# Delta rule: the 16x16 substitution issued on GpSimd, and diagonal blocks taken to scratch by eight small DMAs

## The chip, the core and the metric

The kernel runs on one core of a Trainium2 chip. The metric is device time in microseconds for one launch, that is, one inference step of a two-layer recurrent trunk. Engines have short names in the profile: PE is TensorE (PEld its weight loads), DVE is VectorE, ACT is ScalarE, POOL is GpSimd, SP is the engine that issues nearly all DMAs (its queue is SPq).

## The reference, cut to what matters

The step takes 2048 prompt tokens and 8 sample tokens of width 1024 through an even layer (gated linear attention beside a state-space model) and then an odd layer, the gated delta rule. Only the odd layer matters here. For each of 8 heads and each chunk of tokens it computes

```python
kk = einsum('bhik,bhjk->bhij', ki, ki)
lower = where(strict, bi[..., :, None] * kk * decay, 0.0)
sol = triangular_solve(lower + eye, rhs, left_side=True, lower=True, unit_diagonal=True)
u_v, w_k = sol[..., :DN_DV], sol[..., DN_DV:]
v_new = u_v - einsum('bhik,bhkv->bhiv', w_k, S)
o = einsum('bhik,bhkv->bhiv', qi * exp(gcum)[..., None], S) + einsum('bhij,bhjv->bhiv', scores, v_new)
S = S * exp(g_last)[..., None] + einsum('bhjk,bhjv->bhkv', ki * exp(g_last - gcum)[..., None], v_new)
```

So a unit lower triangular matrix is inverted per chunk and head, and the state S passes from chunk to chunk.

## The kernel before, in words

The 2048 tokens of the odd layer are 16 chunks of 128 tokens. Four chunks make a block (the first block also carries the 8 sample tokens), and a block is worked head by head: 4 blocks x 8 heads are 32 steps, numbered g. The kernel works with chunks of 128 where the reference has 64; the result is the same.

A step has these parts, each a Python generator that issues instructions and yields:

- `dn_dense` projects keys, queries, values and the gate for the head (matmuls `pmm` on TensorE with weights `whl` that SP loads at line 308 into a ring of four buffers), with a convolution on VectorE (line 1687) and the tail of the block kept by GpSimd (line 1680).
- `dn_prefix` loads the decays into the single buffer `gr` (line 1740, issued by SP), makes the decay matrix `E` (VectorE line 1743, GpSimd mask line 1744, ScalarE), the norms of the keys (a power on GpSimd, line 1727), and the scaled triangular matrix `MT`, 128 x 4 x 128 (line 1779). It then begins the inverse: the eight 16x16 blocks on the diagonal of `MT` are brought together for all partitions and solved by substitution.
- `dn_queries` makes the norms of the queries (lines 1726, 1727, 1815), turns the values, and scales the queries by `eg` on GpSimd (line 1831). `eg` lies in the buffer of `gr`, so the next step's load at line 1740 waits for line 1831.
- `dn_inverse` expands the solved blocks to `U` and its transpose `Tm` (lines 1841 and 1845), and doubles the block size three times, 16 to 32, 64 and 128, with small matmuls `prc` that alternate with copies on VectorE (lines 1859, 1861, 1882) and ScalarE.
- `dn_chain` passes the state `dS` through the four chunks (matmuls `pch` and `ppo`; VectorE lines 1916 and 1933), and `dn_gate` gates the result.

Between blocks `dn_entry` norms the next block's input (GpSimd products of 128x1024 at line 641), and `dn_out` multiplies by the output weights (sums at lines 2038 and 2091).

The substitution in `dn_prefix` goes as follows before the change. VectorE multiplies `MT` by a mask of diagonal blocks into `X` (line 1784, the buffer `lb`) and sums `X` over the eight blocks into `md`, 16 numbers per row and chunk (line 1786). One DMA writes `md` to scratch in DRAM (line 1788, two scratch tensors used in turn), and two DMAs read it back into two tiles LB, buffers `la` and `lb`, such that each partition holds all 16 rows of its block (line 1791). Then `u_` is filled with the unit rows (line 1794), and 15 times a row product (line 1798) and a sum (line 1800) follow, each on 128 partitions x 4 chunks x 15 down to 1 columns; each operation needs the one before it. Both are VectorE's.

What sets the order: TensorE's instructions are placed by hand. `Weave` switches between the generators and counts TensorE's time; a part that needs a result waits for a posted key and its delay (`LAT["mt"]` is 28.3 us from `MT` to the inverse). All other engines' instructions are ordered when the kernel is built, by a planner with a simulated time line and priorities (`LEAD` gives the chain and the side parts theirs), and on the chip each engine works its list strictly in that order, waiting where it must.

Of the kernel before, what the change touches and what calls it, by code (L numbers as in the profile page):

```python
# [12 lines left out]
F32 = mybir.dt.float32  # L13
# [5 lines left out]
OP = mybir.AluOpType  # L19
AX = mybir.AxisListType  # L20
# [3 lines left out]
P = 128  # L24
# [115 lines left out]
def tile_trunk(ctx, tc, A, O):  # L140
    nc = tc.nc
# [8 lines left out]
    NCG = GBLK[0][1]  # L150

    def bounds(blk):
        c0, n = blk
        first = c0 == 0
        ns = NSM if first else 0
        off = 0 if first else NSM + P * c0
        subs, c = [], 0
        o = 0
        np_ = -(-(P * n + ns) // 512)
        while c < n:  # L160
            k = -(-(n - c) // (np_ - len(subs)))
            w = P * k + (ns if c == 0 else 0)
            subs.append((o, w, c, k))
            o += w
            c += k
        return ns, off, o, subs
# [21 lines left out]
    def ptp():  # L188
        return psum.tile([P, 512], F32, tag="tp", bufs=2, name="ptp")

    def prc():
        return psum.tile([P, 512], F32, tag="rc", bufs=2, name="prc")
# [39 lines left out]
    blkd = const.tile([P, P], F32, name="blkd")  # L232
    posd = const.tile([P, 16], F32, name="posd")

    def delta_masks():
# [5 lines left out]
                                fill=0.0, base=15, channel_multiplier=-1)  # L241
        nc.vector.tensor_reduce(posd, ident.rearrange("p (b i) -> p i b", i=16), axis=AX.X, op=OP.add)

# [1077 lines left out]
    def s5_glu(sp, half):  # L1321
# [64 lines left out]
        if ns:  # L1386
# [14 lines left out]
    dp = Phase(tc, "dn", late=("Oh", "Ol", "on", "og", "kq_", "U", "Tm", "zz", "la", "lb", "xx", "ww", "sw", "so",  # L1401
                               "ktok", "vtok"))
# [313 lines left out]
    def tiles_of(n):  # L1716
        return lambda tag, bufs=1: dp.tile([P, NCG, P], F32, tag=tag, bufs=bufs, name=tag)[:, :n]

    def norms(pt, n, name):

        ss = dp.tile([P, NCG], F32, tag=name, bufs=2, name=name)[:, :n]
        for c in range(n):
            jk = dp.tile([P, P], BF16, tag="jk", bufs=1, name="jk")
            nc.scalar.activation(jk, pt[:, c * P:(c + 1) * P], AF.Square, accum_out=ss[:, c:c + 1])  # L1724
        rn = dp.tile([P, NCG], F32, tag="rn" + name, bufs=2, name="rn")[:, :n]
        nc.vector.tensor_scalar(ss, ss, 4.0 * EPS, None, op0=OP.add)
        nc.gpsimd.tensor_tensor(rn, ss, mhalf.to_broadcast([P, n]), op=OP.pow)
        return ss, rn

    def dn_prefix(dp, blk, h, g):  # L1730

        ns, off, T, subs = bounds(blk)
        n = blk[1]
        kT = dd[g][0]
        bcol, neg, bs = gates[blk]
        b3 = lambda t: t.unsqueeze(2).to_broadcast([P, n, P])
        mb = lambda m: m.unsqueeze(1).to_broadcast([P, n, P])
        T3 = tiles_of(n)
        gr = dp.tile([P, TG], F32, tag="gr", bufs=1, name="gr")
        nc.sync.dma_start(gr[:, :T], gc_d[h:h + 1, off:off + T].to_broadcast([P, T]))  # L1740
        c3 = lambda t: t[:, ns:T].rearrange("p (c t) -> p c t", t=P)
        E = T3("E")
        nc.vector.tensor_tensor(E, c3(gr), b3(bcol[:, :n, 32 + h]), op=OP.subtract)
        nc.gpsimd.affine_select(E, E, pattern=[[0, n], [1, P]], compare_op=OP.is_ge,
                                fill=-1e30, base=0, channel_multiplier=-1)
        nc.scalar.activation(E, E, AF.Exp)
        eg = gr
        nc.scalar.activation(eg[:, :T], gr[:, :T], AF.Exp)
        if ns:
            egs[g] = dp.tile([P, NSM], F32, tag="egs", bufs=2, name="egs")  # L1750
            nc.vector.tensor_copy(egs[g], eg[:, :NSM])
            weave.post(("eg", g))
        egl = dp.tile([P, NCG], F32, tag="egl", bufs=3, name="egl")[:, :n]
        nc.vector.tensor_copy(egl, c3(eg)[:, :, P - 1])

        ktok = T3("ktok", 3)
        pt = ptp()
        for c in range(n):
            pe.transpose(pt[:, c * P:(c + 1) * P], kT[:, c], ident)
        sk, rk = norms(pt, n, "sk_")  # L1760
        nc.vector.tensor_tensor(ktok, pt[:, :n * P].rearrange("p (c t) -> p c t", t=P),
                                E[:, :, P - 1:P].to_broadcast([P, n, P]), op=OP.mult)
        ivr = dp.tile([P, NCG], F32, tag="ivr", bufs=2, name="ivr")[:, :n]
        nc.vector.scalar_tensor_tensor(ivr, sk, 0.5, rk, op0=OP.mult, op1=OP.mult)
        cb = dp.tile([P, NCG], F32, tag="cb", bufs=3, name="cb")[:, :n]
        nc.vector.tensor_tensor(cb, rk, rk, op=OP.mult)
        nc.vector.tensor_tensor(cb, cb, bcol[:, :n, h], op=OP.mult)
        ncb = dp.tile([P, NCG], F32, tag="ncb", bufs=2, name="ncb")[:, :n]
        nc.vector.tensor_scalar(ncb, cb, -1.0, None, op0=OP.mult)
        keys[g] = c3(eg), E, ktok, ivr, cb, egl  # L1770
        weave.post(("keys", g))
        yield LAT["tp"]

        pk = prc()
        for c in range(n):
            pe.matmul(pk[:, c * P:(c + 1) * P], kT[:, c], kT[:, c], start=True, stop=True)
        MT = T3("MT", 2)
        for c in range(n):
            nc.vector.scalar_tensor_tensor(MT[:, c], pk[:, c * P:(c + 1) * P], ncb[:, c:c + 1],  # L1779
                                           E[:, c], op0=OP.mult, op1=OP.mult)  # L1780


        X = T3("lb")
        nc.vector.tensor_tensor(X, MT, mb(blkd), op=OP.mult)
        md = dp.tile([P, NCG, 16], F32, tag="md", bufs=1, name="md")[:, :n]
        nc.vector.tensor_reduce(md, X.rearrange("p c (b i) -> p c i b", i=16), axis=AX.X, op=OP.add)  # L1786
        w = md_d[g % 2]
        nc.sync.dma_start(w[:, :n * 16], md.rearrange("p c i -> p (c i)"))
        LB = [dp.tile([P, 8, NCG * 16], F32, tag=t, bufs=b, name="LB")[:, :, :n * 16] for t, b in (("la", 1), ("lb", 1))]
        for i in range(2):  # L1790
            nc.sync.dma_start(LB[i], bass.AP(w.tensor, w.offset + i * 8 * NCG * 16,
                                             [[16 * NCG * 16, 8], [0, 16], [NCG * 16, 8], [1, n * 16]]))
        u_ = dp.tile([P, NCG, 16], F32, tag="u_", bufs=2, name="u_")[:, :n]
        nc.vector.tensor_copy(u_, posd.unsqueeze(1).to_broadcast([P, n, 16]))
        t_ = dp.tile([P, NCG, 16], F32, tag="t_", bufs=1, name="t_")[:, :n]
        for j in range(15):
            L3 = LB[j // 8][:, j % 8].rearrange("p (c i) -> p c i", i=16)
            nc.vector.tensor_tensor(t_[:, :, j + 1:], L3[:, :, j + 1:],
                                    u_[:, :, j:j + 1].to_broadcast([P, n, 15 - j]), op=OP.mult)
            nc.vector.tensor_tensor(u_[:, :, j + 1:], u_[:, :, j + 1:], t_[:, :, j + 1:], op=OP.add)  # L1800
        mid[g] = MT, u_
        weave.post(("mid", g), LAT["mt"])

# [168 lines left out]
    def dn_sample(dp, h, kqs, eg, bs, oh, ol, zs):  # L1972
# [37 lines left out]
        nc.vector.tensor_tensor(jk, sk[:, 0], sk[:, 1], op=OP.mult)  # L2010
        nc.vector.tensor_reduce(qk, jk, axis=AX.X, op=OP.add)
        o = dp.tile([NSM, P], F32, tag="so", bufs=1, name="so")
# [225 lines left out]
    def prefixes():  # L2238
        yield "rsd", len(SBLK) - 1
        sp.close("sq")  # L2240
        gp.close("ext", "out2", "out")
        dp.open("late", "right")
        oo[GBLK[0]] = new_o()
        for g, blk, h in steps:
            if h == 0:
                yield "gates", g // NH
                columns(dp, blk, bac[blk])
            if g > 1:
                yield "prefix", g - 2
            if g > 2:  # L2250
                yield "chain", g - 3
            if g:
                yield "queries", g - 1
            yield "k", g
            yield from dn_prefix(dp, blk, h, g)
# [32 lines left out]
    a, b = LEAD  # L2288
# [34 lines left out]
```

## Time and profile before

| | |
|---|---|
| median of 3 runs | 3323.97 us (3307.7, 3323.97, 3343.99) |
| profiled execution | 3307.6 us, its span 3305.7 us, mean granted TensorE clock 0.962 |
| TensorE busy | 2975.1 us (90%), 18425 matmuls |
| VectorE busy | 2214.6 us (67%), 5715 instructions |
| ScalarE busy | 1256.0 us (38%) |
| GpSimd busy | 952.5 us (29%), 1204 instructions |
| substitution steps | 32, the first `MT` at 1742.6 us, the last `Tm` of line 1845 at 3233.1 us |

The span is from the first to the last instruction of the profiled execution; the time also has what lies around it. Busy shares are means over stages with different limits, so what a stage waits for has to be read from that stage. An arrow in a row names what ended an engine's idle time. The chain of work that ended last has 3% of the span in the loads of LB from scratch and 2% in the writes of `md`.

### The profile page before, as it was taken

Reading aid. Unit: us, or ns where it says so; the run is one execution under the profiler, and the core shown is the slowest. Engines: PE = TensorE matmul, PEld = TensorE weight load, DVE = VectorE, ACT = ScalarE, POOL = GpSimd, SP = SyncE. Lnnn points to the kernel's source line nnn. Section 1 sums busy time; section 2 is a strip of 40 time slices with the busy share of each in tenths; the row PEclk is TensorE's granted clock in tenths of the full one; section 3 lists DMA queues with packets and bytes.
Section 4 is the critical chain, followed back from the end, with each engine's and each line's share of the span. In section 5 each row is a group of like instructions: output and inputs, shape, how many; then the busy total and the mean of one; then the engine's idle time right before and its main releaser. Section 6 shows DMA issues by size and latency. Waiting matters only on the chain.

```text
span 3305.7 us, 52923 instructions
## 1 busy us (share of the span) xinstructions
PE 2975.1 (90%) x18425; PEld 2510.2 (76%) x18425; DVE 2214.6 (67%) x5715; ACT 1256.0 (38%) x3321; POOL 952.5 (29%) x1204
## 2 busy tenths in 40 slices
PE   6888899899999979879988988889999899999998
PEld 6777677677778858777778888877777688777876
DVE  7766666635535448657658888667775777757775
ACT  5343343333323223331244444434444344434442
POOL 6565344322112231330234344421111111211111
PEclk9999999999999989999998899999999999999999
DMA  7576955763563474574476566674446644474445
GB/s 215 183 221 194 299 160 151 234 214 128 179 224 125 155 266 151 177 249 130 145 236 205 158 186 200 199 255 142 132 129 195 217 129 135 128 253 142 144 128 184
DMA packets 398871, 602.94 MB, mean 182 GB/s; under 512 B 61113, under 2 KB 256556, under 8 KB 398468
## 3 DMA queue, kind: packets, MB, share of 16 engines
q1 hardware_dynamic: 398102, 598.39, 57.3%
q8 instruction: 145, 2.38, 0.3%
q10 hardware_dynamic: 502, 1.17, 0.1%
q14 instruction: 122, 1.00, 0.1%
HBM read 433.31 MB, written 166.34 MB: 181 GB/s over the span
## 4 chain that ended last, share of the span: by engine, by line
PE 29%; DVE 15%; DMA 10%; issue 3%; ACT 2%; POOL 2%; SPq 1%; DVEq 0%; POOLq 0%; ACTq 0%
PE pmm L93 20%; PE prc L93 3%; DMA LB<-md_d 3%; PE pch L93 2%; DMA md_d<-md 2%; PE ptp L97 2%; PE ppo L93 2%; DMA gr<-gc_d 1%; DVE yc L1687 1%; DVE z L1242 1%; DMA whl<-split 1%; DVE z L1232 1%; DVE z L1238 1%; DVE MT L1779 1%; DVE md L1786 1%
## 5 line engine op out<-in xcount | busy, mean ns | idle before, releaser
L93 PE MATMUL pmm<-Hh,whl 128*128 128x512 f32 (+4 forms) x5200 | 1602.7, 371 | 32.8 <-ACT Hh L643 10.4
L93 PEld LDWEIGHTS pmm<-Hh,whl 128*128 128x128 f32 x5200 | 954.2, 194 | 164.1 <-ACT Hh L643 12.0
L93 PE MATMUL pmm<-Hl,whl 128*128 128x512 f32 (+5 forms) x2640 | 941.4, 357 | 8.1 <-DVE Hl L644 5.6
L93 PEld LDWEIGHTS pmm<-Hl,whl 128*128 128x128 f32 (+1 forms) x2640 | 508.8, 193 | 58.9 <-DVE Hl L644 7.8
L93 PE MATMUL pmm<-Oh,whl 128*128 128x512 f32 (+2 forms) x1120 | 353.2, 377 | 33.2 <-DVE res L1059 11.4
L315 POOL TENSOR_TENSOR whl<-raw,whl 128x512 fp32r<-128x512 f32 (+1 forms) x176 | 229.7, 1309 | 212.4 <-ACT whl L314 160.4
L93 PEld LDWEIGHTS pmm<-Oh,whl 128*128 128x128 f32 x1120 | 209.3, 198 | 69.5 <-DVE res L1059 14.6
L1687 DVE SCALAR_TENSOR_TENSOR yc<-pre,cvec,yc 128x512 f32<-128x512 f32 (+1 forms) x288 | 229.5, 797 | 37.9 <-ACT yc L1685 34.9
L93 PE MATMUL pmm<-Ol,whl 128*128 128x512 f32 (+2 forms) x560 | 201.8, 360 | 1.4 <-DVE Ol L365 1.4
L314 ACT ACTIVATE whl<-raw 128x512 fp32r<-128x512 f32 (+1 forms) x176 | 108.1, 617 | 71.1 <-PE pmm L93 57.1
L93 PEld LDWEIGHTS pmm<-Ol,whl 128*128 128x128 f32 x560 | 111.3, 199 | 12.1 <-DVE Ol L365 2.4
L902 DVE TENSOR_TENSOR dlt<-b 128x512 f32<-128x512 f32 x112 | 89.9, 803 | 38.5 <-ACT E L909 37.5
L903 ACT ACTIVATE E<-dlt 128x256 f32<-128x256 f32 x112 | 47.4, 423 | 169.9 <-DVE dlt L902 44.4
L1680 POOL COPY halo<-pre 128x3 f32<-128x3 f32 x96 | 20.9, 217 | 298.9 <-ACT pre L1677 297.2
L93 PEld LDWEIGHTS prc<-Tm,MT 32*32 32x32 f32 (+2 forms) x1024 | 67.2, 139 | 51.1 <-DVE Tm L1882 30.1
L1677 ACT ACTIVATE pre<-pmm 128x512 f32<-128x512 f32 (+1 forms) x120 | 61.0, 510 | 115.9 <-PE pmm L93 115.8
L93 PE MATMUL pmm<-oh,whl 128*128 128x512 f32 (+3 forms) x320 | 92.4, 367 | 12.5 <-DVE res L1373 8.1
L641 POOL TENSOR_TENSOR xb<-xb,rr 128x1024 f32<-128x1024 f32 (+1 forms) x32 | 77.6, 2434 | 89.8 <-DMA xb<-xs_d 34.9
L93 PE MATMUL prc<-Tm,MT 32*32 32x32 f32 (+2 forms) x1024 | 75.5, 225 | 30.1 <-DVE Tm L1882 22.8
L1059 DVE TENSOR_TENSOR res<-pmm,res 128x512 f32<-128x512 f32 (+2 forms) x80 | 46.2, 584 | 76.6 <-PE pmm L93 55.9
L1724 ACT ACTIVATE jk<-ptp 128x128 bf16<-128x128 f32 x256 | 70.6, 276 | 67.5 <-PE ptp L97 62.8
L1951 ACT ACTIVATE jk<-ppo,rq 128x128 bf16<-128x128 f32 x128 | 46.7, 365 | 128.7 <-PE ppo L93 127.8
(1526 smaller groups left out, 6032.3 us busy)
## 6 DMA issues: line engine op xcount, KB each, us to landing
whl<-split SPq DMA_DIRECT2D x460, 512.0 KB
split<-whl SPq DMA_DIRECT2D x168, 512.0 KB
res<-xs_d SPq DMA_DIRECT2D x88, 256.0 KB
sm<-s5m SPq DMA_DIRECT2D x32, 514.0 KB
raw<-in_w_in_even SPq DMA_DIRECT2D x32, 512.0 KB
xs_d<-res SPq DMA_DIRECT2D x64, 256.0 KB
raw<-in_w_in_odd SPq DMA_DIRECT2D x32, 512.0 KB
LB<-md_d SPq DMA_DIRECT2D x64, 256.0 KB
```

Of the source, the lines that this page charges most:

```text
L93: return self.e.matmul(out, w, x, **kw)
L97: return self.e.transpose(out, x, ident)
L314: nc.scalar.activation(t[:, 0, :m], raw[:, k:k + m], AF.Copy)
L315: nc.gpsimd.tensor_tensor(t[:, 1, :m], raw[:, k:k + m], t[:, 0, :m].bitcast(F32), op=OP.subtract)
L641: nc.gpsimd.tensor_tensor(xb, xb, rr.unsqueeze(1).to_broadcast(list(xb.shape)), op=OP.mult)
L902: nc.vector.tensor_tensor(d3, b3, b3[:, :, s - 1:s].to_broadcast([P, nb_, 2 * s]), op=OP.subtract)
L903: nc.scalar.activation(E3[:, :, s:], d3[:, :, s:], AF.Exp, scale=IS)
L1059: nc.vector.tensor_tensor(res[:, o:o + w], ps, res[:, o:o + w], op=OP.add)
L1677: nc.scalar.activation(pre[:, X0 + c * P:X0 + (c + k) * P], ps[:, n0:], AF.Copy)
L1687: nc.vector.scalar_tensor_tensor(yv, pre[:, i:W - 3 + i], convw[:, ti, i:i + 1], yv, op0=OP.mult, op1=OP.add)
L1724: nc.scalar.activation(jk, pt[:, c * P:(c + 1) * P], AF.Square, accum_out=ss[:, c:c + 1])
L1951: nc.scalar.activation(jk[:rows], po[:rows, c * P:(c + 1) * P], AF.Square, scale=rq[:rows, c:c + 1], accum_out=s1[:, c:c + 1])
```

## The change

The masked product and the sum over blocks are gone. Eight DMAs, one for each group of 16 partitions, take the 16x16 diagonal blocks of the four chunks from `MT` to the scratch tensor; each moves 16 partitions x 4 chunks x 16 numbers, in pieces of 64 bytes (4 KB in all). The two loads of LB are the same. The copy that fills `u_` and the 30 operations of the substitution are issued on GpSimd. All that reads `u_`, and the rest of the kernel, is unchanged; the tiles `X` and `md` are no longer made.

```diff
-        X = T3("lb")
-        nc.vector.tensor_tensor(X, MT, mb(blkd), op=OP.mult)
-        md = dp.tile([P, NCG, 16], F32, tag="md", bufs=1, name="md")[:, :n]
-        nc.vector.tensor_reduce(md, X.rearrange("p c (b i) -> p c i b", i=16), axis=AX.X, op=OP.add)
         w = md_d[g % 2]
-        nc.sync.dma_start(w[:, :n * 16], md.rearrange("p c i -> p (c i)"))
+        for b in range(8):
+            nc.sync.dma_start(w[16 * b:16 * b + 16, :n * 16].rearrange("p (c i) -> p c i", i=16),
+                              MT[16 * b:16 * b + 16, :, 16 * b:16 * b + 16])
         LB = [dp.tile([P, 8, NCG * 16], F32, tag=t, bufs=b, name="LB")[:, :, :n * 16] for t, b in (("la", 1), ("lb", 1))]
         for i in range(2):
             nc.sync.dma_start(LB[i], bass.AP(w.tensor, w.offset + i * 8 * NCG * 16,
                                              [[16 * NCG * 16, 8], [0, 16], [NCG * 16, 8], [1, n * 16]]))
         u_ = dp.tile([P, NCG, 16], F32, tag="u_", bufs=2, name="u_")[:, :n]
-        nc.vector.tensor_copy(u_, posd.unsqueeze(1).to_broadcast([P, n, 16]))
+        nc.gpsimd.tensor_copy(u_, posd.unsqueeze(1).to_broadcast([P, n, 16]))
         t_ = dp.tile([P, NCG, 16], F32, tag="t_", bufs=1, name="t_")[:, :n]
         for j in range(15):
             L3 = LB[j // 8][:, j % 8].rearrange("p (c i) -> p c i", i=16)
-            nc.vector.tensor_tensor(t_[:, :, j + 1:], L3[:, :, j + 1:],
+            nc.gpsimd.tensor_tensor(t_[:, :, j + 1:], L3[:, :, j + 1:],
                                     u_[:, :, j:j + 1].to_broadcast([P, n, 15 - j]), op=OP.mult)
-            nc.vector.tensor_tensor(u_[:, :, j + 1:], u_[:, :, j + 1:], t_[:, :, j + 1:], op=OP.add)
+            nc.gpsimd.tensor_tensor(u_[:, :, j + 1:], u_[:, :, j + 1:], t_[:, :, j + 1:], op=OP.add)
```

## Rows read from the trace of the kernel before

**Rows 1.** Busy us by stretches: stretch, length, PE, PEld, DVE, ACT, POOL, clock, DMA.

```profile
1740.00:3306.00 1566.00, 1428.30 (x9599) 1212.40 (x9597) 1146.98 (x3166) 647.39 (x1886) 355.45 (x417) 0.96 0.55 171
1740.00:2130.00 390.00, 342.07 (x2828) 320.65 (x2827) 327.35 (x950) 174.29 (x547) 170.93 (x177) 0.93 0.61 188
2220.00:2470.00 250.00, 235.96 (x1596) 195.58 (x1595) 188.53 (x534) 104.38 (x314) 34.92 (x51) 0.99 0.47 143
```

**Rows 2.** Waits of TensorE, 1740 to 3306 us: total, times, longest.

```profile
PE pch L93 <- DVE dS L1933: 23.0, 13, 4.9
PE prc L93 <- DVE Tm L1882: 22.8, 18, 1.9
...
PE pmm L93 <- DVE yt L2091: 9.2, 10, 2.7
...
PE prc L93 <- DVE Tm L1859: 7.3, 7, 2.3
...
PE pch L93 <- DVE u__27195 L1800: 4.2, 1, 4.2
```

**Rows 3.** Tile LB: what ended its engine's standing, us and times.

```profile
  DMA LB<-md_d: 72.3, 31
```

**Rows 4.** Time line, 2270 to 2320 us: start, us, instruction, [idle before, releaser].

```profile
2279.51 0.22 DVE L1798 TENSOR_TENSOR t__23762<-LB,u__23760 128x60 f32<-128x60 f32 x1 [2.55 <-DMA LB<-md_d]
...
2280.27 0.28 DVE L1882 COPY Tm<-prc 32x128 f32<-32x128 f32 x1
...
2280.61 0.68 PE L93 MATMUL prc<-Tm,MT 64*64 64x64 f32 x8 [1.21 <-DVE Tm L1882]
```

**Rows 5.** Time lines of DVE and PE: Tm made, then first used.

```profile
1822.18 0.71 DVE L1845 STREAM_TRANSPOSE Tm<-U 128x512 f32<-128x512 f32 x1
1829.88 1.00 PE L93 MATMUL prc<-Tm,MT 128*128 128x64 f32 x8
...
2292.48 0.71 DVE L1845 STREAM_TRANSPOSE Tm<-U 128x512 f32<-128x512 f32 x1
2306.05 1.00 PE L93 MATMUL prc<-Tm,MT 128*128 128x64 f32 x8
```

**Rows 6.** Groups of DVE instructions, 1740 to 3306 us: busy us, mean ns, idle.

```profile
L1786 DVE TENSOR_REDUCE md<-lb 128x64 f32<-128x512 f32 x32 | 33.1, 1034 | 0.5
...
L1784 DVE TENSOR_TENSOR lb<-MT,blkd 128x512 f32<-128x512 f32 x32 | 23.5, 736 | 0.1
```

**Rows 7.** Busy time of line 1798 alone: stretch, length, DVE, clock, DMA.

```profile
1740.00:3306.00 1566.00, 112.64 (x480) 0.96 0.55 171
```

**Rows 8.** Time lines of POOL and DVE at the end of a block.

```profile
2475.88 7.04 POOL L641 TENSOR_TENSOR xb<-xb,rr 128x1024 f32<-128x1024 f32 x3 [1.81 <-ACT rr L1571]
...
2476.22 2.09 DVE L1798 TENSOR_TENSOR t__25812<-LB,u__25810 128x36 f32<-128x36 f32 x1
...
2480.71 2.26 DVE L1798 TENSOR_TENSOR t__25812<-LB,u__25810 128x32 f32<-128x32 f32 x1
```

**Rows 9.** Time line of SP's queue in the step of rows 4.

```profile
2273.35 0.32 SPq L1788 DMA_DIRECT2D md_d<-md  x1
...
2275.56 1.23 SPq L1791 DMA_DIRECT2D LB<-md_d  x2
```

**Rows 10.** Waits of SP's queue, 1740 to 3306 us.

```profile
SPq L308 <- PE pmm L93: 474.5, 161, 10.0
...
SPq L1740 <- POOL qT L1831: 68.0, 18, 8.8
```

**Rows 11.** Two GpSimd lines: ns min/median/max, first and last start.

```profile
L590 POOL TENSOR_TENSOR x<-q x64: 393/405/1207, 132.5 to 689.2; 128x128 f32<-128x128 f32 x64
...
L593 POOL COPY smR<-q x64: 173/184/1012, 130.8 to 680.8; 128x1 f32<-128x1 f32 x64
```

**Rows 12.** POOL's time line in the step of rows 4; DVE's standing at line 1743.

```profile
2282.97 1.28 POOL L1831 TENSOR_TENSOR qT<-qT,gr 128x512 f32<-128x512 f32 x1 [10.56 <-DVE sq__23893 L1726]
...
2289.27 0.64 POOL L1744 TENSOR_SCALAR_AFFINE_SELECT E<-E 128x512 f32<-128x512 f32 x1 [4.06 <-DVE E L1743]
...
  DMA gr<-gc_d: 29.2, 25
```

## The prediction

> **What bounds the kernel now.** I read the busy time by stretches first. The code that changes runs in the delta-rule half, 1740 to 3306 us. There TensorE is busy 1428 of 1566 us, so 138 us are all that any change off TensorE can win, 4% of the run; VectorE is busy 1147 us and GpSimd 355 us [rows 1]. The reader is to see two different parts in it: up to 2130 us (the first block of tokens) VectorE is busy 327 of 390 us and GpSimd 171, while in the steady steps (2220 to 2470 us) TensorE has 236 of 250 us and GpSimd only 35.
>
> Then the waits of TensorE, because only these are time. The largest that end with VectorE are 23.0 us for the state dS, 22.8 us for Tm at line 1882, 9.2 for the output sum, 7.3 for Tm at line 1859 and 4.2 at one place where a substitution operation was the last releaser [rows 2]: 66.5 us in these rows, of which I look for what the change can reach.
>
> The third view is the tile that the substitution reads. VectorE stood 72.3 us, in 31 of 32 steps, at its first substitution operation, until the load of LB had landed [rows 3]. VectorE works its list in order, so what is behind stands too. One step shows it: the first operation comes at 2279.51 after 2.55 us of standing, line 1882 only after it at 2280.27, and the matmuls that need Tm start at 2280.61 after a wait of 1.21 us [rows 4]. So the substitution reaches TensorE by what stands behind it on VectorE, and not by its own result: Tm from line 1845 is done at 2293.19 (2292.48 + 0.71) and first multiplied at 2306.05, 12.9 us later. In the tightest of the 32 steps the pair is 1822.89 and 1829.88, 7.0 us [rows 5].
>
> **The change part by part.** The sum is made against the profiled execution, 3307.6 us (a span of 3305.7 and 1.9 around it). The median of the three runs is 3323.97, 16.4 higher; I take the same difference off both.
>
> *Masked product and sum go.* 23.5 us and 33.1 us of VectorE [rows 6]. *Thirty small operations a step leave VectorE*, with one copy: line 1798 alone is busy 112.6 us in 480 operations, 0.235 us each [rows 7]; line 1800 has as many of like shape, so I put the whole at some 225 us. Together about 280 of VectorE's 1147 us. As busy time that is worth nothing by itself; it counts where TensorE waits for VectorE.
>
> *The standing at LB leaves VectorE.* What hangs behind it are the waits at lines 1882 and 1859, 22.8 + 7.3 = 30.1 us, and the 4.2 us one: 34 us gained. The ratio 30.1 / 72.3 = 0.42 is my price for one microsecond of standing on VectorE; I use it below.
>
> *Block ends.* There a large GpSimd product holds up VectorE: three products of 2.35 us run from 2475.88 to 2482.92, and the substitution operations on VectorE, which elsewhere last 0.2 us, last 2.09 and 2.26 us there, the first and the last of three [rows 8]. They cannot stand on VectorE any more; I take 5 us for the block ends. Gains: 39 us.
>
> *Eight small DMAs in place of one.* Issue to issue, the old one has landed and let the LB load start after 2.21 us, and that load is used 3.95 us after its issue [rows 9]. An issue costs SP 0.32 us, so eight are 2.6 us; the last should land about 2.2 us after its own issue. From MT to the substitution that adds some 2.3 us of issues and takes away 0.69 + 1.03 us of work on VectorE. The net of some 0.6 us is hidden by the 7.0 to 12.9 us above: 0. SP mostly stands for buffers of weights (line 308 waiting for TensorE, 474.5 us in all), so its 2.3 us a step are taken from that [rows 10]: 0 again, and at worst 2.3 x 32 x 0.42 = 31 us if SP's cover were gone. A gain from it I exclude: nothing waits for less.
>
> *The substitution on GpSimd.* No row has this operation there. From below: a copy of one column takes 0.184 us; from above: a product of 128 columns, twice the widest of the thirty, takes 0.405 us [rows 11]. The widths are 60 down to 4, so I take 0.30 with the gap to the next: 9 us a step (5.5 to 12.2), against the 13 us in which VectorE works through them now among other work. By its length alone it is covered by the slack, even at the upper end.
>
> The Trainium skill would price it higher. Its page "GPSIMD Engine Reference", section "4.1 Engine selection", says that two-input elementwise work belongs on VectorE and is about twice as slow on GpSimd. By it an operation would take an estimated 0.47 us, and a step 14 us. The trace does not show it so far: rows 7 and 11 leave room for 0.8 to 1.7 times.
>
> *What is queued on GpSimd behind it.* In the same stretch GpSimd multiplies the queries (line 1831, 2282.97, 1.28 us), raises the norms to a power (line 1727) and masks E for the next step (line 1744, 2289.27) [rows 12]. Line 1831 is the one that matters: it releases the only buffer gr, for which SP stands at line 1740 already (68.0 us, 18 times [rows 10]) and VectorE at line 1743 (29.2 us, 25 times [rows 12]). There is no slack: each microsecond by which line 1831 comes later stands on SP and on VectorE. Now it runs 3.5 us after LB has landed; in the new list some of the thirty will be in front of it, by the planner's order. At 0.30 us 12 of them fit in 3.5 us; if the planner puts 15 there, it is 1 us late. I take 1 us: 31 x 1 x 0.42 = 13 us lost. Bounds: 0 (all that is in front fits) and, with all thirty in front at 0.30, 9 - 3.5 = 5.5 us late, 72 us.
>
> *Both engines at SBUF together.* Rows 8 show that a VectorE operation can last until a GpSimd one is over. Ahead, each of thirty short ones can do this to VectorE: about five such meetings a step at 0.3 us would be 32 x 5 x 0.3 x 0.42 = 20 us. Against it stand the 280 us taken off VectorE. I count 0, bounds minus 16 (rival 1) and plus 20.
>
> Sum: 39 - 13 = 26 us gained; 3307.6 becomes 3282 and the median **3298 us**.
>
> **Rivals.**
> 1. *VectorE's relief thins the other waits as well.* With a quarter of its work gone, half of the waits for dS and for the output sum (23.0 + 9.2) go, 16 us, and GpSimd is never late: 39 + 16 = 55, so 3269 us. For it: VectorE at 327 of 390 us in the first block. Against: in the steady steps it has 25% of idle time and the waits are there all the same.
> 2. *Slower: the queue on GpSimd sets gr free late.* Place: line 1831, and from it SP at 1740 and VectorE at 1743. It decides from the point where 31 x lateness x 0.42 is above 39 us, which is 3.0 us. At the upper price, 0.405 us, with all but four of the thirty in front, 26 x 0.405 - 3.5 = 7 us of lateness give 91 - 39 = 52 us lost: 3376 us. For it: no slack in rows 10 and 12, and GpSimd's 171 us of 390 in the first block, to which 72 would be added. Against: line 1831 would be ordered by when its inputs are ready, between two dependent operations. The Trainium skill's page named above is on this side.
> 3. *The standing only moves*, from LB on VectorE to gr and to the norms that VectorE takes from GpSimd, and gain and loss cancel: 3324 us. For it: GpSimd stands for the same LB, with line 1831 behind it.
> 4. *The eight DMAs do not overlap*: 8 x 2.2 = 18 us in place of 2.2, 15.5 more, beyond the 12.9 us of slack by 2.6 in a usual step: 32 x 2.6 = 83 less 39, 3368 us. Against: the two loads of LB are issued back to back in 1.23 us and both are there within 3.95 [rows 9]. The Trainium skill speaks for it: "DMA: Bandwidth & Descriptors", section "Rules for kernel authors", wants many small transfers joined into one, since below 64 KB one pays mostly overhead; these are 4 KB each.
>
> **How the numbers follow.** Chances: forecast 0.32, rival 1 0.27, rival 2 0.24, rival 3 0.13, rival 4 0.04. The spread of the three runs is 1.1%, so a change within 1% (33 us) is what a measurement here can't tell from none. Faster than 3291: all of rival 1 and 0.06 of the forecast, 0.33. Slower than 3357: 0.22 of rival 2 and 0.03 of rival 4, 0.25. The rest, 0.42, is within 1%. The range goes from 3245 (rival 1 with all of the dS waits gone and a little of the rest) to 3385 (just past rival 2); beyond it I leave some 0.07 below and 0.11 above. The forecast's own range is 3285 to 3318.
>
> **What would show it.** VectorE's busy time from 1740 us on should fall from 1147 to some 860 us and GpSimd's rise from 355 to about 640; the wait for LB should be GpSimd's, TensorE's waits at lines 1882 and 1859 under 8 us together; the thirty operations at 0.2 to 0.3 us each, and Tm still 5 us or more ahead of its use. Rival 2 shows as SP's wait at 1740 well over 68 us and VectorE's at 1743 over 100; rival 3 as such waits of some 70 us beside unchanged waits of TensorE; rival 4 as the substitution beginning over 15 us after MT. The forecast is wrong if an operation on GpSimd takes over 0.4 us, or if TensorE's waits for dS grow.

## The result, and the profile after

The changed kernel takes 3360.2 us (median of 10 runs, 3347.99 to 3370.21) against 3329.31 us of before in the same comparison (10 runs): the ratio is 1.0096, with a 95% interval of 1.007 to 1.0121, some 31 us slower where the prediction had 26 us faster. The ratio is within the 1% that the prediction could not tell from none, but with ten runs each the interval excludes no change as well as any gain; the time itself lies just past 3357 us, above which the prediction had a chance of 0.25. The profiled run took 3347.99 us, its span is 3346.0 us and the mean granted clock 0.955 (before 0.962); both profiled runs are the fastest of their kernel, and lie 40.4 us apart. Lines behind the change have numbers lower by two: 1798 is now 1796, 1815 is 1813, 1831 is 1829, 1845 is 1843, 1859 is 1857, 1882 is 1880, 1916 is 1914 and 1933 is 1931.

Busy time by stretches, columns as in [rows 1]:

```profile
1740.00:3306.00 1566.00, 1417.92 (x9549) 1203.89 (x9548) 905.43 (x2073) 639.48 (x1870) 632.71 (x1403) 0.96 0.55 168
1740.00:2130.00 390.00, 333.36 (x2735) 314.50 (x2734) 262.88 (x672) 167.38 (x534) 233.78 (x422) 0.92 0.58 180
```

The work moved as intended: VectorE is busy 905 us where it was 1147, GpSimd 633 where it was 355. Nothing is gained by that alone. The waits of TensorE from 1740 us to the end (total, times, longest), to be held against [rows 2]:

```profile
PE pch L93 <- DVE dS L1931: 26.8, 18, 3.9
PE prc L93 <- DVE Tm L1843: 13.4, 4, 4.9
...
PE pmm L93 <- DVE yt L2089: 9.1, 6, 2.6
...
PE prc L93 <- DVE Tm L1857: 5.7, 5, 2.8
...
PE pch L93 <- DVE xx__28643 L1914: 3.1, 1, 3.1
...
PE pch L93 <- DVE xx__24406 L1914: 2.9, 1, 2.9
```

Of the 22.8 us at line 1882 only 0.4 are left, and line 1859 fell from 7.3 to 5.7 us: what was predicted of them came. In their place stand two others. The tiles `xx` of line 1914, of which two rows are shown, make 38.2 us together (7.3 before), and Tm of line 1843, for which TensorE had no wait before, makes 13.4 us in four. All rows of this view sum to 149.7 us after and 125.4 before, 24.3 us more.

Where the 40.4 us lie is seen when both traces are cut at the same work, the start of the first `MT` (1742.63 us before, 1751.21 after) and of the ninth, where the second block begins. TensorE's list is the same in both. Stretch, length, PE, clock, DMA; before, then after:

```profile
1742.63:3305.70 1563.07, 1425.67 (x9577) 0.96 0.55 171
1742.63:2182.23 439.60, 388.89 (x3114) 0.94 0.62 193
...
1751.21:3346.00 1594.79, 1433.18 (x9577) 0.96 0.55 168
1751.21:2208.22 457.01, 394.28 (x3114) 0.92 0.60 186
```

So 8.6 us have come up ahead of the first `MT`, where the change does nothing (mean granted clock there 0.954 after, 0.964 before). The delta rule itself is 31.7 us longer: 24.2 us in which TensorE waits and 7.5 us of its busy time. Of the 31.7, 17.4 are in the first block, at a clock of 0.92 against 0.94, and 14.3 in the three others.

What `xx` waits for is seen in VectorE's own waits:

```profile
DVE rq L1813 <- POOL rn L1727: 92.2, 27, 6.1
DVE E L1743 <- DMA gr<-gc_d: 74.7, 29, 4.8
```

Before, the first of these was 0.4 us in 2 waits, and the second 29.2 us in 25 [rows 12]. And GpSimd, at its first substitution operation (line 1796), stood until LB had landed; where VectorE had 72.3 us in 31 steps [rows 3], it has

```profile
  DMA LB<-md_d: 253.6, 32
```

One steady step shows how these belong together (time line: start, us, instruction, idle before and releaser; it is of the same kind as that of [rows 4, 9, 12], two heads further on):

```profile
2374.98 5.12 SPq L1785 DMA_DIRECT2D md_d<-MT  x8
...
2381.37 1.28 SPq L1789 DMA_DIRECT2D LB<-md_d  x2
...
2385.30 0.17 DVE L1726 TENSOR_SCALAR sq__24747<-sq__24747 128x4 f32<-128x4 f32 x1 [2.00 <-ACT jk L1724]
...
2387.07 0.30 POOL L1796 TENSOR_TENSOR t__24624<-LB,u__24622 128x60 f32<-128x60 f32 x1 [10.07 <-DMA LB<-md_d]
...
2388.58 0.28 POOL L1796 TENSOR_TENSOR t__24624<-LB,u__24622 128x52 f32<-128x52 f32 x1
...
2388.82 1.01 POOL L1727 TENSOR_TENSOR rn<-sq__24747,mhalf 128x4 f32<-128x4 f32 x1
...
2389.87 0.26 DVE L1813 TENSOR_SCALAR rq<-rn 128x4 f32<-128x4 f32 x1 [3.08 <-POOL rn L1727]
2390.04 0.34 DVE L1914 SCALAR_TENSOR_TENSOR xx__24805<-pch,neg,vtok 128x128 f32<-128x128 f32 x1
2390.07 1.27 POOL L1829 TENSOR_TENSOR qT<-qT,gr 128x512 f32<-128x512 f32 x1
...
2390.53 0.46 PE L93 MATMUL pch<-xx__24805,U 128*128 128x128 f32 x2 [0.85 <-DVE xx__24805 L1914]
...
2391.36 0.32 SPq L1740 DMA_DIRECT2D gr<-gc_d  x1
...
2395.29 0.69 DVE L1743 TENSOR_TENSOR E<-gr,bcol 128x512 f32<-128x512 f32 x1 [4.32 <-DMA gr<-gc_d]
...
2395.90 0.34 DVE L1931 SCALAR_TENSOR_TENSOR dS<-dS,egl,pch 128x128 f32<-128x128 f32 x1
...
2396.30 0.49 PE L93 MATMUL pch<-dS,kT 128*128 128x128 f32 x2 [2.08 <-DVE dS L1931]
```

The sums of the query norms are ready at 2385.47. Their power (line 1727) stands behind five substitution operations in GpSimd's list, and the first of these stands for LB until 2387.07; so it runs at 2388.82, 3.35 us after its input. Before, in the step of [rows 12], it was done at 2285.21, 0.93 us ahead of line 1815, and no `xx` stood directly behind that line:

```profile
2284.20 1.01 POOL L1727 TENSOR_TENSOR rn<-sq__23893,mhalf 128x4 f32<-128x4 f32 x1
...
2285.88 0.34 DVE L1916 SCALAR_TENSOR_TENSOR xx__23961<-pch,neg,vtok 128x128 f32<-128x128 f32 x1
2286.14 0.16 DVE L1815 TENSOR_SCALAR rq<-rn 128x4 f32<-128x4 f32 x1
```

Now VectorE, working its list in order, stands 3.08 us at line 1813, which needs it, with `xx` behind: TensorE waits 0.85 us. The scaling of the queries (line 1829) is as late, `gr` is issued only at 2391.36, VectorE stands 4.32 us at line 1743 with the state's update behind it, and TensorE waits 2.08 us. The standing at LB is on GpSimd now, and costs by what is listed behind it there. LB itself is late because the eight issues take 5.12 us of SP, 0.64 each.

Over the 32 steps the substitution starts 12.5 us after MT is made (9.9 before; means, from the time lines). Tm then stands ready 8.2 us ahead of its use in place of 12.0; in four steps of the first block it has no slack left, and these are the 13.4 us. There the substitution, with GpSimd's other work between its operations, lasts 24.3 us from its first operation to its last (mean of eight steps), where it lasted 17.2 on VectorE.

### The profile page after: what moved, and what is told of

It reads as the page before. It is cut to its first block, busy times and chain, and to the rows that moved or that the text cites. A ratio compares the mean times of both kernels' runs of the same rounds, so it can differ in the third digit from the quotient of the medians.

```text
span 3346.0 us, 53072 instructions
## 1 busy us (share of the span) xinstructions
PE 2990.2 (89%) x18425; PEld 2519.3 (75%) x18425; DVE 1989.5 (59%) x4659; ACT 1255.0 (38%) x3321; POOL 1234.9 (37%) x2196
## 5 line engine op out<-in xcount | busy, mean ns | idle before, releaser
L93 PE MATMUL pmm<-Oh,whl 128*128 128x512 f32 (+2 forms) x1120 | 355.8, 380 | 37.8 <-DVE res L1059 10.1
L93 PEld LDWEIGHTS pmm<-Ol,whl 128*128 128x128 f32 x560 | 112.7, 201 | 11.9 <-DVE Ol L365 2.3
L93 PEld LDWEIGHTS prc<-Tm,MT 32*32 32x32 f32 (+2 forms) x1024 | 66.9, 138 | 41.4 <-DVE Tm L1843 14.3
L93 PE MATMUL prc<-Tm,MT 32*32 32x32 f32 (+2 forms) x1024 | 75.6, 225 | 20.6 <-DVE Tm L1843 13.4
L1245 POOL COPY hst<-z 128x1 f32<-128x1 f32 x64 | 12.6, 196 | 209.5 <-DVE z L1244 178.4
```

The source lines that it names most:

```text
L93: return self.e.matmul(out, w, x, **kw)
```

## The experiments

My theory after the comparison was that the standing at LB costs on GpSimd by what is listed behind it, the query norms above all. The rivals: LB's being later costs in itself, by Tm; or GpSimd's other work in the first block does; or SP's issues. The expectations call them by letters, each explained where it stands; in e1 to e4 theory A is the list behind LB, B the first block and C the DMAs, and from e9 on C is the list and D the later LB. Each ratio is to the kernel before on the same chip, with its 95% interval.

**e1: the eight DMAs alone**; the copy and the thirty operations stay on VectorE. The edit is against the changed kernel.

```diff
-        nc.gpsimd.tensor_copy(u_, posd...
+        nc.vector.tensor_copy(u_, posd...
...
-            nc.gpsimd.tensor_tensor(t_[:, :, j + 1:], ...
+            nc.vector.tensor_tensor(t_[:, :, j + 1:], ...
...
```

> The eight small DMAs alone, the substitution on VectorE as before. Theory A (GpSimd stands for LB with the query norms of line 1727 queued behind it; VectorE then stands for these norms at line 1813, with line 1914 behind it, for which TensorE waits): the loss of the changed kernel (3360 against 3329 us) is not here, 3320 to 3340 us. Theory C (the DMAs: the substitution begins 12.1 us after MT in place of 8.9, so whoever waits for LB stands 3 us longer in each of 32 steps): a third of the loss or more is here, 3340 to 3360 us, and VectorE's standing for LB grows from 72 to some 150 us.

Measured: 3341.56 us against 3326.59, ratio 1.0046 (1.0026 to 1.0067), 15 us slower although the masked product and the sum, 56.6 us of VectorE, are gone. The substitution starts 12.7 us after MT, and VectorE stands 121.4 us for LB in place of 72.3. That is at the near end of theory C's range, and the prediction's "0" for the DMAs falls.

**e2: the move alone**; masked product, sum and the one DMA as before, the copy and the thirty operations on GpSimd (the last lines of the change's diff, on the kernel before).

> The substitution on GpSimd alone, with the masked product, the sum and one DMA as before. Theory A, and theory B (in the first block GpSimd's weight splits of line 315 stretch the substitution until Tm is late): nearly all of the loss is here, 3350 to 3365 us, with VectorE's waits at the line that takes the query norms at 60 us or more. Theory C: the loss shrinks to a third or less, 3330 to 3340 us.

Measured: 3308.61 against 3326.59, ratio 0.9948 (0.9932 to 0.9964), 17 us faster; the start is 10.1 us after MT. VectorE already stands there at the query norms:

```profile
DVE E L1743 <- DMA gr<-gc_d: 91.9, 28, 8.1
DVE rq L1815 <- POOL rn L1727: 64.7, 27, 4.3
```

None of the theories had a gain here. Nor does the trace show where the 17 us are: the two profiled executions are equal (3307.2 and 3307.6 us, both at a granted clock of 0.962), and TensorE's waits sum to 129.3 us against 125.4. What differs is the clock over all runs, 0.957 to 0.962 (median 0.960) against 0.950 to 0.962 (median 0.956); why it is higher, no run shows.

The parts do not add: minus 17 and plus 15 would be no change, and together they give plus 31. So about 33 us come of one meeting the other.

**e3: line 1813 to GpSimd**, so that VectorE does not stand for the query norms itself.

```diff
-        nc.vector.tensor_scalar(rq_, rq, P ** -0.5, None, op0=OP.mult)
+        nc.gpsimd.tensor_scalar(rq_, rq, P ** -0.5, None, op0=OP.mult)
```

> The changed kernel with the scaling of the query norms (line 1813) issued on GpSimd too, so that nothing on VectorE waits for them there. Theory A: the 92 us of standing at line 1813 and the waits of TensorE for line 1914 (some 35 us in all) go, 3325 to 3340 us. Theories B and C: it stays within 10 us of the changed kernel, 3350 to 3365 us.

Measured: 3367.57, ratio 1.0124 (1.0098 to 1.015), no better than the changed kernel. VectorE's standing went to line 1743 for `gr`, 148.5 us in 30 waits (74.7 after), and TensorE's waits for dS to 56.9 us. Theory A as it stood had 3325 to 3340. The one instruction on VectorE was not the cause; whatever comes next on VectorE that hangs on GpSimd takes its place.

**e4: the first block on VectorE**, the eight DMAs in all blocks.

```diff
+        eng = nc.vector if g < NH else nc.gpsimd
-        nc.gpsimd.tensor_copy(u_, posd...
+        eng.tensor_copy(u_, posd...
...
```

> The changed kernel with the substitution on VectorE in the eight steps of the first block and on GpSimd in the 24 others. Theory B: the 14 us that the changed kernel lost over the first block go, 3340 to 3348 us, and TensorE's 13.4 us of waits for Tm after the substitution with them. Theory A alone: only the share of the first block in the standing at line 1813 goes, at most 7 us, 3353 us or more.

Measured: 3345.39, ratio 1.0054 (1.0032 to 1.0077), some 14 us below the changed kernel, though the two intervals overlap. The traces agree on the place: the first block, from the first `MT` to the ninth, takes 445 us where it took 457 (440 before). There GpSimd has weight splits (line 315) among the thirty operations and Tm comes too late. The rest of the loss is elsewhere.

**e5 and e6: seven idle DMAs in the kernel of e2**, in e5 behind the two loads of LB (SP busy, LB not later), in e6 in front of the DMA that LB waits for. The diff is e6's; in e5 the source of the seven is MT.

```diff
+        for b in range(1, 8):
+            nc.sync.dma_start(mx_d[g % 2][16 * b:16 * b + 16, :n * 16], md[16 * b:16 * b + 16].rearrange("p c i -> p (c i)"))
         nc.sync.dma_start(w[:, :n * 16], md.rearrange("p c i -> p (c i)"))
```

> The substitution on GpSimd with the masked product, the sum and one DMA (e2), and seven further DMAs of the new shape (16 partitions of MT to another scratch, read by nobody) issued behind the two loads of LB. The substitution starts as early as in e2, and SP has some 4 us more to issue in each step. Theory C1 (the loss is the later start: all who stand for LB stand 2.4 us longer): as e2, 3303 to 3318 us. Theory C2 (the loss is SP's time, the weights and gr that SP issues come later): most of the loss is here, 3335 us or more.

> As e5, but the seven further DMAs (16 partitions of the summed tile to another scratch) are issued in front of the one that LB waits for; their issues should put the start of the substitution off by 2 us or more. Theory C1: a large part of the 50 us between e2 and the changed kernel comes back, 3330 to 3360 us. Theory C2: as in e5. Theory C3 (neither; the order that the planner makes for eight DMAs, or the short pieces): 3303 to 3318 us in both.

Measured: e5 3320.04 against 3332.82, ratio 0.9978 (0.9955 to 1.0001): that is between the two theories; the issues on SP cost about 10 us against e2, if anything (the intervals overlap), and VectorE's standing at the query norms is unchanged, 64.7 us. e6 is the surprise: 3295.35, ratio 0.9893 (0.9859 to 0.9928), faster than e2, though its substitution starts at 13.6 us, later than in the changed kernel. So a kernel with a later LB need not be slower; no theory had this. GpSimd stood for LB only 114.9 us in 21 steps, and VectorE at the query norms 26.8 us. What sets it apart is GpSimd's list: in most steps of e6 the query norms stand in front of the first substitution operation, in the changed kernel behind five to seven of the thirty, in e2 behind nine to eleven (steps 10 to 15).

**e7: LB without a wait**; it is loaded from a constant scratch tensor, so the inverse is of other data than the reference's.

```diff
-            nc.sync.dma_start(LB[i], bass.AP(w.tensor, w.offset + ...
+            nc.sync.dma_start(LB[i], bass.AP(mc_d.tensor, mc_d.offset + ...
```

> The changed kernel, but LB is loaded from a scratch that is written once and not in the step (the inverse of other data is left out of the result), so the substitution waits for no MT; the eight DMAs are still issued. Theory C1: all that stood for LB goes, 3280 to 3310 us, and the waits for the query norms with it. Theory C2: SP has the same issues, 3340 us or more.

Measured: 3259.37, ratio 0.9786 (0.9752 to 0.982), with TensorE's waits at 94.0 us. All eight DMAs and all thirty operations on GpSimd are in it: what the wait for LB costs in all its ways is at most 0.031 of the time, some 103 us, against the changed kernel (without it the planner lets the substitution run 102 us ahead of MT in the mean, which moves other work too).

**e8: e2 with the first block on VectorE.**

> The substitution on GpSimd with the masked product, the sum and one DMA (e2), but on VectorE in the eight steps of the first block. Theory B (the weight splits of line 315 stretch the substitution there; e4 was 15 us below the changed kernel): 3290 to 3302 us, below e2 by 7 to 15 us. If e4 won only because VectorE, in place of GpSimd, took the later start: as e2, 3303 to 3315 us, or slower.

Measured: 3308.68, ratio 0.9933 (0.9908 to 0.9958), as e2. With LB early, and the list in e2's order, GpSimd is no loss in the first block.

**e9: the norms first.** The eight DMAs and GpSimd as in the change, but the first substitution operation has to follow the query norms.

```diff
+        t0 = pe.t
+        yield "nq", g
         u_ = dp.tile([P, NCG, 16], F32, tag="u_", bufs=2, name="u_")[:, :n]
+        nc.gpsimd.tensor_copy(u_[:, :, 0], nq[g])
         nc.gpsimd.tensor_copy(u_, posd...
...
-        weave.post(("mid", g), LAT["mt"])
+        weave.posted[("mid", g)] = t0 + LAT["mt"]
...
         nc.vector.tensor_scalar(rq_, rq, P ** -0.5, None, op0=OP.mult)
+        nq[g] = rq
+        weave.post(("nq", g))
```

TensorE's list is the same; in GpSimd's, lines 1727 and 1836 (the scaling of the queries) come ahead of all thirty operations in each of the 32 steps. VectorE's list differs mainly in that U and Tm stand a few places later.

> The kernel after, eight DMAs kept; the first substitution operation is made to follow the norms of the queries (line 1727) by a small copy of these norms into u_, which the unit rows then overwrite. In GpSimd's list the norms and the scaling of the queries then stand in front of all thirty operations in every step. Theory C (what costs is the work listed behind GpSimd's standing for LB): VectorE's standing at the query norms falls from 92 to under 30 us, GpSimd's standing for LB from 254 to under 150, and the time goes to the level of the move alone or below, 3295 to 3315 us where before is about 3328. Theory D (what costs is that LB is there 2.4 us later, by way of the later Tm): the time stays at 3340 to 3360.

Measured: 3306.01 against 3323.05 (17 runs), ratio 0.9949 (0.993 to 0.9969), 0.0147 or some 49 us below the changed kernel. Its substitution starts later still, 14.4 us after MT, and Tm has 5.1 us of slack in place of 8.2. A step of it, one head ahead of the changed kernel's shown above:

```profile
2339.34 5.06 SPq L1785 DMA_DIRECT2D md_d<-MT  x8
...
2350.44 0.16 DVE L1726 TENSOR_SCALAR sq__24316<-sq__24316 128x4 f32<-128x4 f32 x1
...
2350.68 1.01 POOL L1727 TENSOR_TENSOR rn<-sq__24316,mhalf 128x4 f32<-128x4 f32 x1 [9.29 <-DVE sq__24316 L1726]
...
2351.66 1.29 POOL L1836 TENSOR_TENSOR qT<-qT,gr 128x512 f32<-128x512 f32 x1
2351.72 1.25 DVE L1818 TENSOR_SCALAR rq<-rn 128x4 f32<-128x4 f32 x1 [0.30 <-POOL rn L1727]
...
2353.45 0.29 POOL L1799 TENSOR_TENSOR t__24333<-LB,u__24330 128x60 f32<-128x60 f32 x1
...
2357.42 0.69 DVE L1743 TENSOR_TENSOR E<-gr,bcol 128x512 f32<-128x512 f32 x1 [3.60 <-DMA gr<-gc_d]
...
2358.03 0.34 DVE L1938 SCALAR_TENSOR_TENSOR dS<-dS,egl,pch 128x128 f32<-128x128 f32 x1
...
2358.43 0.49 PE L93 MATMUL pch<-dS,kT 128*128 128x128 f32 x2 [0.25 <-DVE dS L1938]
```

The power runs 0.08 us after its input is done (2350.60), VectorE stands 0.30 us, TensorE waits 0.25 us for dS where it was 2.08, and not at all for `xx`. Over all steps GpSimd's standing for LB is

```profile
  DMA LB<-md_d: 18.8, 6
```

and VectorE's for the query norms 7.8 us in place of 92.2. VectorE still stands 81.4 us for `gr`, so the total of that standing does not tell the two kernels apart, and for U it stands no less than in the changed kernel (45.1 against 37.6 us). From the first `MT` on the trace is 49.5 us shorter than the changed kernel's, by 30 us of TensorE's waits and 19.4 us of its busy time (mean granted clock 0.965 against 0.956). All of it is in the three later blocks; the first takes 459 us against 457. So for those three blocks it is shown that the order around the standing at LB is the cause; why the planner chose the other order, no run shows. What is left is the first block (1740 to 2130 us):

```profile
PE prc L93 <- DVE Tm L1850: 24.0, 5, 8.7
PE pch L93 <- DVE xx__18209 L1921: 5.5, 1, 5.5
```

**e10: the same order in e2. e11: e9 with the first block on VectorE. e12: both**, masked product, sum and one DMA, the first block on VectorE, the norms first in the others.

> The same order in the kernel with the masked product, the sum and one DMA, and the substitution on GpSimd. Theory C: as there is still some 65 us of standing at the query norms with the move alone (ratio 0.995), another 10 to 20 us are gained, 3288 to 3300 us; the eight DMAs then cost little against it (under 10 us between this run and the one with eight DMAs). Theory D: no change from the move alone, 3309.

> The kernel after with the norms first, and in the first block of tokens the substitution on VectorE. Theory C with a second part (in the first block, where GpSimd has other work between the thirty operations, Tm comes with no slack): some 10 to 15 us below the run with the norms first alone, since its waits at line 1845 of before's numbering go. If the order alone was the cause in the first block too: no difference.

> Masked product, sum and one DMA as before; the substitution on VectorE in the first block of tokens, on GpSimd with the norms of the queries first in the other three. Against the run with eight DMAs and the same division of the blocks (3280 us, ratio 0.988). If eight DMAs cost time in themselves, as the 15 us between the two runs with the norms first on GpSimd throughout suggest, this one is the lower, 3265 to 3275 us. If that difference came from the first block alone, by a substitution on GpSimd that came too late for Tm, both are the same, 3275 to 3290; and where VectorE is the tighter engine in the first block, as its busy share says, this one with its masked product and sum there is the slower by some 5 us.

Measured: e10 3291.37, ratio 0.9912 (0.9888 to 0.9935); e11 3279.84, 0.9876 (0.9848 to 0.9903); e12 3274.06 against 3329.86, 0.9835 (0.9801 to 0.9869), the fastest of all but e7, and faster than both kernels. The order gains 0.0036 in e10 against e2, where LB comes earlier and less stood behind it (the two intervals just overlap). The first block on VectorE gains 0.0073 in e11 and 0.0077 in e12 now that the norms are first: TensorE's waits for Tm in that block fall from 24.4 us to 5.3 and 9.2, and the block, from the first `MT` to the ninth, is 22.2 and 19.4 us shorter. Eight DMAs in place of the sum and one DMA cost 0.0037 (e9 against e10) and 0.0041 (e11 against e12), 12 to 14 us as in e1 and near the 10 us of e5; but in each of these two pairs the intervals overlap, and what waits for SP's issues in them was not traced further.

## Why the prediction was wrong, by its steps

The sum was 39 us gained and 13 lost, 26 us faster. By the runs the move alone is worth 17 us, the DMAs cost 15 where 0 stood, and 33 us that the sum did not have come of the two together.

**The thirty operations on GpSimd: right singly, too short as a step.** They last 0.30 us at 60 columns and 0.21 at 4, and start 0.38 to 0.29 us apart, against the 0.30 taken with the gap. On VectorE line 1798 has a mean of 0.235 us [rows 7]. The factor of two of the Trainium skill's page "GPSIMD Engine Reference", section "4.1 Engine selection", is not seen at these widths (means over all steps 0.285 and 0.236 us). But a step takes 11.9 to 15.5 us in steady steps and 24.3 in the first block, against the 9 (5.5 to 12.2) forecast, for GpSimd's other work stands between the operations.

**The standing leaves VectorE: right as to its waits, not as to the gain.** Lines 1882 and 1859 fell from 30.1 to 6.1 us. But already in e2 other waits took their place (129.3 us in all against 125.4), so its 17 us cannot be put down to these 34.

**Block ends at 5 us: not seen.** GpSimd's products of line 641 now stand between the substitution's operations, which there take 26.7 and 26.9 us where they took 22.8 and 23.9. What VectorE gained by it, no run separates.

**The eight DMAs at 0: the step that failed first.** The issue was priced at 0.32 us, from the DMA of `md`, which moves whole rows. But a dearer issue was in the same view: the two loads of LB, whose pattern is not plain rows, take 1.23 us, 0.62 each [rows 9], and the new ones take 0.59 (median), 5.1 us for eight from first to last in place of 2.6. The start came 2.6 us later where 0.6 was forecast. Then the text hid the delay under the slack of Tm, 7.0 to 12.9 us [rows 5]. That slack covers who uses the result. It does not cover what is listed behind the engine that waits for the input; and the prediction had used this very thing for VectorE, where it priced a microsecond of standing at 0.42. Its worst case of 31 us looked for the harm at SP. The Trainium skill's rule on joining small transfers ("DMA: Bandwidth & Descriptors", section "Rules for kernel authors") points the right way, and e1 agrees with 15 us; the transfers did overlap, though, so rival 4's 18 us in a row were wrong, and the cost seen is issue time on SP and what waits behind LB.

**The queue on GpSimd at 13 us: the step that decided.** It counted substitution operations in front of line 1831, starting from where LB had landed before. It left out that GpSimd would stand for LB as VectorE had (253.6 us), and it named the power of line 1727 without pricing it. That one has little slack, 0.93 us in the step of [rows 12]; it was enough before, when VectorE waited 0.4 us in all at line 1815. In the step shown the power is 3.35 us late, and `xx` and dS hang behind VectorE's standing: 34.7 us more of TensorE's waits (38.2 + 26.8 against 7.3 + 23.0). The count itself was not the error: in steps 10 to 15 only five to seven operations are in front, where up to 12 were to be harmless. Rival 3, the standing only moves, is what happened; it was given the right places, `gr` and the norms, but a price equal to the gain. Rival 2's mark, VectorE's standing at line 1743 over 100 us, did not show (74.7), and e9 says why that was the wrong mark: with 81.4 us there it is 49 us faster.

**Tm 5 us or more ahead of its use: wrong** in the first block, where GpSimd's other work lengthens the substitution and LB is late (13.4 us of waits; 17.4 of the 31.7 us are in this block), and at two block ends, where 1.8 and 1.4 us are left.

**Rival 1, all of VectorE's relief: not seen.** VectorE is busy 242 us less in the stretch of [rows 1], and the waits for dS and for the output sum, of which half were to go, are 26.8 and 9.1 us where they were 23.0 and 9.2.

## What to carry to other kernels

Moving a waiting instruction to another engine moves its standing too: list what stands behind it on the new engine, ask which of that has no slack, and place that first; here the place in one list was worth 49 us, and the moved work itself 17 at most. Slack of a result says nothing of the neighbours of the one who waits for the input. The price of a DMA's issue is taken from the row of like shape, not from the nearest in place, and parts that nearly cancel apart (minus 17, plus 15) are tried together before they are added.

## What the runs showed of the hardware that was not expected

SP took 0.32 us to issue the DMA of whole rows (line 1788 before, 0.319 to 0.320 us from the smallest to the median) and 0.59 us for 16 partitions of four 64-byte pieces, although the latter move an eighth of the bytes. The idle DMAs of e6, which move whole rows of 16 partitions, took 0.42 us (median).

In two places a small operation on one of GpSimd and VectorE lasted longer while the other ran a large one, once in each direction. In e9's step the 128x4 operation of line 1818 lasts 1.25 us and ends at 2352.97, with GpSimd's product at 2352.95; in the changed kernel it lasts 0.26 us in the step shown. In that step of the changed kernel GpSimd's operation of 24 columns lasts 0.69 us, against 0.24 for those on either side of it, and stands beside VectorE's product of line 1743 (2395.29 to 2395.98):

```profile
2395.06 0.24 POOL L1798 TENSOR_TENSOR u__24622<-u__24622,t__24624 128x28 f32<-128x28 f32 x1
...
2395.38 0.69 POOL L1796 TENSOR_TENSOR t__24624<-LB,u__24622 128x24 f32<-128x24 f32 x1
...
2396.67 0.24 POOL L1798 TENSOR_TENSOR u__24622<-u__24622,t__24624 128x24 f32<-128x24 f32 x1
```

That the one held up the other is read from the times alone, and what such meetings cost in all was not measured.
